# A decoder trunk on one core: first weights into the scan's buffer, the first norm's squares behind the first tiles, both broadcasts of the even mixer placed later

## The chip, the core and the metric

The kernel runs on one core of one Trainium2 chip. Its work is spread over TensorE (PE, with its weight loads shown as PEld), VectorE (DVE), ScalarE (ACT), GpSimd (POOL) and SyncE (SP), which issues most of the DMAs; a few are issued by ACT. Each engine takes its instructions strictly in the order in which they stand in its queue, and waits on semaphores for the others. The metric is the time of one execution in device microseconds.

## The reference, cut to what matters

A two-layer decoder trunk over 256 tokens of width 2048, in float32, batch 1. The first ("even") layer's mixer is where the change lies:

```python
def conv_ssm_mixer(h, w_in, conv_w, ..., w_out):
    z = h @ w_in                                   # 2048 x 4096
    gate_b, gate_c, xa, u = jnp.split(z, ...)      # four parts of 1024
    ya = gate_b * causal_dwconv(gate_c * xa, conv_w)
    ys = s5_branch(u, ...)                         # a complex diagonal scan over the 256 tokens
    return jnp.concatenate([ya, ys], axis=-1) @ w_out

mem_n = rms_norm(mem, norm_mem)                    # 256 memory tokens, used by both layers
for l in range(2):
    h = h + mixer(rms_norm(h, norm_mix[l]))        # even: conv_ssm_mixer, odd: window attention
    h = h + memory_cross_attention(rms_norm(h, norm_xattn[l]), mem_n, w_q, w_kv, w_o)
    h = h + conv_gated_mlp(rms_norm(h, norm_ffn[l]), ...)
return rms_norm(h, norm_final)
```

## The kernel before

All activations are held transposed, 16 slices (k0 to k15) of 128 features by 256 tokens. Matmuls are exact in float32 by splitting: an activation is stored as a pair (high part, rest) side by side in 512 columns, an "op"; a weight is cast by ACT to its high part (`hi`, L90) and DVE subtracts to get the rest (`lo`, L91). One output tile of 128 features is 16 matmuls of `hi` against 512 columns (L105), then 16 of `lo` against 256 (L110). Weights come from memory in pieces of 1 MB into three `raw` buffers; `hi` and `lo` have four buffers each, so two tiles' worth. When a tile is done, `add_halves` copies one half from PSUM on ACT (L160) and adds the other on DVE (L161).

A norm is not applied to the activations before the matmul: the squares of h are summed aside (ACT squares, POOL adds, L172 and L174), PE sums over partitions (L186), DVE takes a reciprocal root in a chain of tiny steps (L194 to L203), builds a diagonal matrix in two halves (L212), PE multiplies it with ones so that every partition gets the factor (L214, the "broadcast"), and ACT copies the result to `rbc` (L216).

The even mixer runs in this order:

- first tiles: the first four output tiles of u (the S5 input) at once, k by k in steps of 1, 1, 2, 2, 2, 4, 4 slices, so that PE can begin when the first slice of x and of the weights `ev_u0` has landed (L259, L262). Squares of h run beside them, four slices late;
- n4 to n7, the other four tiles of u. In n4's follow-up stand the first norm's sum, in n5's its broadcast, then the scaling of u by it (L555), and the splitting of the memory tokens `memT` into ops (16 of them, after n6 and n7);
- for each layer, the memory's keys and values: 16 K tiles (k0 to k15 for layer 0, written k'0 to k'15 here for layer 1), then 16 V steps. K results are gathered four tiles at a time in one buffer, `kst`, and then written to memory by a DMA on ACT's queue (L309). There is one `kst` buffer. Along layer 0's K tiles goes the memory's own norm: tokens loaded after k2, squares after k5 and k6, the reciprocal root after k8, the broadcast after k10;
- 24 gate tiles of w_in, and then the output projection.

The S5 scan (`s5`, four blocks) runs beside all K, V and gate tiles: it is written as a generator, and after each tile `after` lets it emit as many of its steps as a budget per tile allows (S5_US, S5_V, S5_G). A step's heavy rows are DVE's (L493 to L496), ACT's (L489) and a few PE matmuls. The code is written in this order, and a list scheduler turns it into one queue for each engine; the order in the queue is fixed when the program is built. The tile with the tag "S" in the S5 pool has one buffer that holds, one after the other, memT, the memory tokens and the state of every second scan block.

Of the kernel before, what the change touches and what calls it, by code (L numbers as in the profile page):

```python
# [22 lines left out]
P = 128  # L23
# [13 lines left out]
class Trunk:  # L37
# [40 lines left out]
    def wload(self, src, kt, n):  # L78

        nc = self.nc  # L80
        raw = self.rawp.tile([P, kt * n], F32, name="raw", tag="raw")
        nc.sync.dma_start(raw.rearrange("p (k n) -> p k n", n=n), src)
        kc = 1024 // n
        parts = []
        for c in range(0, kt, kc):
            m = min(kc, kt - c)
            hi = self.hip.tile([P, m * n], F32R, name="hi", tag="hi")
            lo = self.lop.tile([P, m * n], F32R, name="lo", tag="lo")
            s = raw[:, c * n:(c + m) * n]
            nc.scalar.copy(hi, s)  # L90
            nc.vector.tensor_tensor(lo, s, hi.bitcast(F32), op=ALU.subtract)  # L91
# [27 lines left out]
    def gemm(self, src, n_tiles, ops, K, evac, late=0, pre=0, mid=None, mid2=None, after=None, one=False, half=None, end=None):  # L119
# [6 lines left out]
        def start(i, k1):  # L126
            n = n_tiles[i]
            w = self.wload(src(n), K, P)
            ps = self.pp.tile([P, 512], F32, name="ps", tag="ps")
# [95 lines left out]
    def setup(self):  # L225
# [15 lines left out]
        def load_x(k0, k1):  # L241
            nc.sync.dma_start(self.hc[:, k0:k1, :], I["xT"][:, k0:k1, :])
        return load_x

    def first_tiles(self, load_x, xs):

        ps = [self.pp.tile([P, 512], F32, name="ps", tag="ps") for _ in range(4)]
        self.stat_begin()
        lag = 4
# [14 lines left out]
        for k in range(KT - lag, KT):  # L264
            self.stat_add(self.h[k])
# [273 lines left out]
    def even_mixer(self):  # L539
# [3 lines left out]
        with tc.tile_pool(name="s5", bufs=1) as pool:  # L543
# [13 lines left out]
            ps = self.first_tiles(load_x, xs)  # L557
# [3 lines left out]

            def load_mem(c):
# [3 lines left out]
            def mem_step(k0, k1):  # L566
                for k in range(k0, k1):
                    self.memop.append(self.split_gain(mem[:, k, :], self.gain(G_MEM, k)))

            def after_u(n):  # L570
                nonlocal rbc
                if n == 4:
                    self.stat_col()
                    load_mem(0)
                elif n == 5:
                    rbc, _ = self.stat_bc()
                    load_mem(1)
                    scale_u(range(0, 6))
                elif n == 6:
                    mem_step(0, 8)  # L580
                    scale_u((6,))
                else:
                    scale_u((7,))
                    mem_step(8, 16)
            rbc = None
            self.gemm(lambda n: win(24 + n), range(4, 8), xs, KT, evac_u, after=after_u)
            r2 = self.smp.tile([P, T], F32, name="r2", tag="r2", bufs=1)
            nc.vector.tensor_tensor(r2, rbc, rbc, op=ALU.mult)
# [4 lines left out]
            def mem_norm(n):  # L593
                if n == 2:
# [4 lines left out]
                elif n in (5, 6):  # L599
                    b = n - 5  # L600
                    nc.scalar.activation(mt["S"][:, b, :], mt["S"][:, b, :], AF.Square, accum_out=mt["ss"][:, b:b + 1])
                elif n == 8:
# [17 lines left out]
            def after_k(n):  # L620
                mem_norm(n)
                after(n)
            self.kv = [self.mem_kv(l, pool, after if l else after_k, after) for l in range(2)]
# [478 lines left out]
```

## Time and profile before

| what | us |
|---|---|
| median of 3 runs | 2818.43 |
| the three runs | 2815.97, 2818.43, 2819.57 |
| the profiled execution | 2817.71 |
| its span, first to last instruction | 2815.9 |
| PE busy in the span | 2785.6 (99%) |
| DVE busy | 1975.3 (70%) |
| ACT busy | 1570.8 (56%) |
| mean granted clock of TensorE | 0.997 |

Where PE is busy nearly all the time, one looks for the places at which it isn't: the list of what PE waits for, and then PE's timeline around the longest entries. An idle time of DVE or ACT costs something only where PE waits for what they bring. A row of a timeline gives the start, the length, the engine and line, what is written and read, the shapes, how many of one kind follow each other, and in brackets the idle time before it and what ended it.

### The profile page before, as it was taken

The page shows a single profiled execution, that of the slowest core. Times are in us where ns is not written, and L with a number is a line of the kernel's source. Part 1 is how long each engine was busy: PE and PEld are TensorE (multiplying, and loading weights), DVE is VectorE, ACT ScalarE, POOL GpSimd, SP SyncE. Part 2 cuts the span into 40 slices and gives each one's busy share as a digit, 9 for nine tenths or more (in the row PEclk, how much of TensorE's full clock was granted, in tenths as well). Part 3 has the DMA queues.
Part 4 walks back from the last instruction along what each step waited for, and adds up shares of the span by engine and source line. Part 5 has one row for each costly group of instructions (what it writes and reads, how often), then busy time and mean ns, then how long its engine had stood idle before and what let it go on. Part 6 is the DMA issues. An engine that isn't in the chain of part 4 may idle for free.

```text
span 2815.9 us, 42249 instructions
## 1 busy us (share of the span) xinstructions
PE 2785.6 (99%) x16263; PEld 2438.2 (87%) x16263; DVE 1975.3 (70%) x3227; ACT 1570.8 (56%) x2544; POOL 360.5 (13%) x397
## 2 busy tenths in 40 slices
PE   9999999999999999999999999999999999999998
PEld 8787878888988888888888888889888888888887
DVE  8978788867666666666666778776666666666666
ACT  7676766655555545545445566555555455454454
POOL 2000000000012211202112310000122022021122
PEclk9999999999999999999999999999999999999999
DMA  8664665555455545455454544454455554554544
GB/s 305 204 213 172 213 226 202 201 181 210 180 177 186 193 171 212 169 206 190 169 210 176 198 171 163 150 211 179 174 185 190 174 205 168 209 192 168 206 171 143
DMA packets 89788, 536.63 MB, mean 191 GB/s; under 512 B 10641, under 2 KB 17137, under 8 KB 38641
## 3 DMA queue, kind: packets, MB, share of 16 engines
q1 hardware_dynamic: 86656, 524.66, 52.7%
q10 hardware_dynamic: 2928, 9.26, 0.9%
q8 instruction: 127, 2.08, 0.3%
q14 instruction: 77, 0.62, 0.1%
HBM read 523.35 MB, written 10.53 MB: 190 GB/s over the span
## 4 chain that ended last, share of the span: by engine, by line
PE 94%; DVE 3%; ACT 2%; DMA 1%; issue 1%; POOL 0%; SPq 0%; DVEq 0%; ACTq 0%; POOLq 0%
PE ps L105 55%; PE ps L110 29%; PE ps L319 2%; PE ps L324 2%; PE ps L320 2%; DVE lo L91 1%; PE m L882 1%; PE m L788 1%; ACT stmp L489 1%; ACT hi L90 1%; DMA kv<-kst 0%; PE m L774 0%; DVE S L494 0%; PE m L742 0%; PE m L852 0%
## 5 line engine op out<-in xcount | busy, mean ns | idle before, releaser
L105 PE MATMUL ps<-op,hi 128*128 128x512 f32 x6997 | 1689.3, 392 | 5.4 <-ACT hi L90 2.8
L105 PEld LDWEIGHTS ps<-op,hi 128*128 128x128 f32 x6997 | 1283.2, 188 | 260.5 <-ACT hi L90 5.2
L91 DVE TENSOR_TENSOR lo<-raw,hi 128x1024 fp32r<-128x1024 f32 (+2 forms) x1033 | 1200.6, 1185 | 378.4 <-ACT hi L90 154.8
L90 ACT CAST hi<-raw 128x1024 fp32r<-128x1024 f32 (+2 forms) x1033 | 1001.8, 983 | 813.0 <-PE ps L105 720.5
L110 PEld LDWEIGHTS ps<-op,lo 128*128 128x128 f32 x7008 | 903.6, 191 | 38.5 <-DVE lo L91 2.3
L110 PE MATMUL ps<-op,lo 128*128 128x256 f32 x7008 | 920.5, 283 | 1.3 <-DVE lo L91 1.3
L172 POOL TENSOR_TENSOR acc<-acc,t 128x256 f32<-128x256 f32 x98 | 90.8, 927 | 1185.7 <-ACT t L174 1181.7
L160 ACT COPY t<-ps 128x256 f32<-128x256 f32 x290 | 106.9, 370 | 166.5 <-PE ps L110 163.6
L919 POOL TENSOR_TENSOR t<-t,rbc 128x256 f32<-128x256 f32 x88 | 68.8, 781 | 748.7 <-DVE t L161 720.9
L922 DVE SCALAR_TENSOR_TENSOR t<-t,ff_conv 128x255 f32<-128x255 f32 x88 | 42.9, 487 | 141.9 <-ACT t L921 141.9
L925 POOL TENSOR_TENSOR t<-t,rbc 128x256 f32<-128x256 f32 x88 | 109.5, 1244 | 216.2 <-ACT t L924 216.2
L68 DVE SCALAR_TENSOR_TENSOR op<-h,gains,op 128x256 fp32r<-128x256 f32 x96 | 72.8, 765 | 85.1 <-ACT op L67 85.0
L489 ACT ACTIVATE stmp<-S,s_pw 128x256 f32<-128x256 f32 (+3 forms) x256 | 116.8, 522 | 27.6 <-DVE S L496 21.6
L75 DVE TENSOR_TENSOR op<-t,op 128x256 fp32r<-128x256 f32 x104 | 43.8, 425 | 118.6 <-ACT op L74 118.2
L161 DVE TENSOR_TENSOR t<-ps,t 128x256 f32<-128x256 f32 x250 | 103.8, 415 | 0.9 <-ACT t L160 0.9
L319 PE MATMUL ps<-hi,op 128*128 128x512 f32 x256 | 101.0, 394 | 0.3 <-ACT hi L90 0.2
L320 PE MATMUL ps<-hi,op 128*128 128x512 f32 x256 | 99.8, 390 | 0.0
L931 POOL TENSOR_TENSOR t<-t 128x256 f32<-128x256 f32 x88 | 67.2, 764 | 135.0 <-DVE t L161 134.7
L74 ACT CAST op<-t 128x256 fp32r<-128x256 f32 x104 | 41.9, 406 | 50.7 <-POOL t L931 43.3
L494 DVE TENSOR_TENSOR S<-S,stmp 128x512 f32<-128x512 f32 (+11 forms) x92 | 60.6, 663 | 13.0 <-ACT stmp L489 12.8
L324 PE MATMUL ps<-lo,op 128*128 128x512 f32 x256 | 63.6, 390 | 0.7 <-DVE lo L91 0.7
L921 ACT ACTIVATE t<-t,ff_b,ff_conv 128x256 f32<-128x256 f32 x88 | 52.3, 595 | 20.7 <-POOL t L919 20.7
(213 smaller groups left out, 1494.9 us busy)
## 6 DMA issues: line engine op xcount, KB each, us to landing
raw<-in_ff_gate SPq DMA_DIRECT2D x88, 1024.0 KB, 4.8
raw<-in_ff_up SPq DMA_DIRECT2D x88, 1024.0 KB, 4.8
raw<-in_ff_down SPq DMA_DIRECT2D x128, 704.0 KB, 4.0
raw<-in_xa_k SPq DMA_DIRECT2D x32, 1024.0 KB, 4.9
raw<-in_xa_v SPq DMA_DIRECT2D x32, 1024.0 KB, 5.3
raw<-in_xa_q SPq DMA_DIRECT2D x32, 1024.0 KB, 4.8
raw<-in_xa_o SPq DMA_DIRECT2D x32, 1024.0 KB, 4.8
raw<-in_ev_w_in SPq DMA_DIRECT2D x28, 1024.0 KB, 4.9
```

Of the source, the lines that this page charges most:

```text
L90: nc.scalar.copy(hi, s)
L91: nc.vector.tensor_tensor(lo, s, hi.bitcast(F32), op=ALU.subtract)
L105: nc.tensor.matmul(ps, lhsT=hi, rhs=o, start=k == 0, stop=False)
L110: self.nc.tensor.matmul(ps[:, :T], lhsT=w[k][1], rhs=ops[k][:, :T], start=False, stop=k == K - 1)
L160: self.nc.scalar.copy(t, ps[:, T:])
L161: self.nc.vector.tensor_tensor(out, ps[:, :T], t, op=ALU.add)
L172: nc.gpsimd.tensor_tensor(self.acc, self.acc, self.sq, op=ALU.add)
L319: nc.tensor.matmul(ps[b], lhsT=o[:, b * P:(b + 1) * P], rhs=w[j][0], start=k == 0, stop=False)
L320: nc.tensor.matmul(ps[b], lhsT=o[:, T + b * P:T + (b + 1) * P], rhs=w[j][0], start=False, stop=False)
L324: nc.tensor.matmul(ps[b], lhsT=self.memop[k][:, b * P:(b + 1) * P], rhs=w[j][1], start=False, stop=k == KT - 1)
L489: nc.scalar.activation(tmp[:, x, :, p - p0, :], at(0, both, p), AF.Copy, scale=pw[:, x, k, 8 * b + p:8 * b + p + 1])
L925: nc.gpsimd.tensor_tensor(y, y, self.rbc, op=ALU.mult)
```

## The change

Four things are done in the even mixer.

- The weights of k0 to k7 of the first tiles land in the S5 pool's "S" tile, which is not in use yet, instead of in the `raw` buffers; so their loads wait for no buffer. x of k0 and k1 is issued by ACT instead of SP.
- The squares of h leave the first tiles. They follow n4 to n7, four in the middle of each; the splitting of memT comes after n5, n6 and n7 instead of n6 and n7, and both loads of memT are issued at once. n4 and n5 accumulate in banks of the other PSUM pool ("m").
- The first norm's sum comes after k0 and its broadcast after k1 of layer 0's K, and all of u is scaled there. The S5 generator starts after k2 instead of k0.
- The memory's norm is moved back by two tiles (loads after k4, squares after k7 and k8, root after k10), and its broadcast goes to layer 1's K, after k'4.

```diff
-    def wload(self, src, kt, n):
+    def wload(self, src, kt, n, raw=None):
-        raw = self.rawp.tile([P, kt * n], F32, name="raw", tag="raw")
+        if raw is None:
+            raw = self.rawp.tile([P, kt * n], F32, name="raw", tag="raw")
...
-            ps = self.pp.tile([P, 512], F32, name="ps", tag="ps")
+            ps = self.pp.tile([P, 512], F32, name="ps", tag="ps") if place is None else place(n)
...
-        def load_x(k0, k1):
-            nc.sync.dma_start(self.hc[:, k0:k1, :], I["xT"][:, k0:k1, :])
+        def load_x(k0, k1, early=False):
+            (nc.scalar if early else nc.sync).dma_start(self.hc[:, k0:k1, :], I["xT"][:, k0:k1, :])
...
-            load_x(k, k + step)
-            w = self.wload(self.I["ev_u0"][:, k:k + step, :], step, 512)
+            load_x(k, k + step, k < 2)
+            w = self.wload(self.I["ev_u0"][:, k:k + step, :], step, 512, room[:, 512 * k:512 * (k + step)] if k < 8 else None)
...
-                if k + j >= lag:
-                    self.stat_add(self.h[k + j - lag])
...
-            ps = self.first_tiles(load_x, xs)
+            ps = self.first_tiles(load_x, xs, place([P, 8 * 512]))
...
+            for c in range(2):
                 nc.sync.dma_start(mem[:, 8 * c:8 * c + 8, :], self.I["memT"][:, 8 * c:8 * c + 8, :])
             self.memop = []
+            self.stat_begin()
+
+            def half_u(n):
+                for k in range(4 * (n - 4), 4 * (n - 3)):
+                    self.stat_add(self.h[k])
+
+            def after_u(n):
+                for k in {4: (), 5: range(0, 5), 6: range(5, 11), 7: range(11, 16)}[n]:
                     self.memop.append(self.split_gain(mem[:, k, :], self.gain(G_MEM, k)))
+            self.gemm(lambda n: win(24 + n), range(4, 8), xs, KT, evac_u, half=half_u, after=after_u,
+                      place=lambda n: self.bank() if n < 6 else self.pp.tile([P, 512], F32, name="ps", tag="ps"))
...
+            def first_norm(n):
                 nonlocal rbc
+                if n == 0:
+                    self.stat_col()
+                elif n == 1:
+                    rbc, _ = self.stat_bc()
+                    scale_u(range(8))
+                    nc.vector.tensor_tensor(r2, rbc, rbc, op=ALU.mult)
...
-                elif n == 10:
-                    self.mrbc, _ = self.stat_bc("mem")
...
             def after_k(n):
+                first_norm(n)
                 mem_norm(n)
+                if n > 1:
+                    after(n)
+
+            def after_k1(n):
+                if n == 4:
+                    self.rcol = self.mcol
+                    self.mrbc, _ = self.stat_bc("mem")
                 after(n)
-            self.kv = [self.mem_kv(l, pool, after if l else after_k, after) for l in range(2)]
+            self.kv = [self.mem_kv(l, pool, after_k1 if l else after_k, after) for l in range(2)]
```

Line numbers shift by a few: the diagonal's rows are L212 before and L213 after, the broadcast L214 and L215, the cast L90 and L91, `lo` L91 and L92, `kst`'s add L161 and L162, the squares L174 and L175.

Three places in the queues. The first is ACT between the first tiles and tile n4; `ps` is the first tiles' sum, `S` holds memT, `h` is x. Before:

```order
L90 CAST hi<-raw 128x1024 [waits DMAHW7_49,DVE_49,PE_49]
L90 CAST hi<-raw 128x1024 [waits DVE_49,PE_49]
L67 ACTIVATE op<-S,gains 128x256 [waits DMAHW0_49]
L67 ACTIVATE op<-S,gains 128x256
L160 COPY t<-ps 128x256 [waits PE_49,Pool_49] x4
L67 ACTIVATE op<-S,gains 128x256 x4
L90 CAST hi<-raw 128x1024 [waits DMAHW1_49,DVE_49]
```

The two casts at the top are tile n4's, the one at the bottom is the first of n5. And now:

```order
L67 ACTIVATE op<-S,gains 128x256 [waits DMAHW0_49]
L67 ACTIVATE op<-S,gains 128x256
L161 COPY t<-ps 128x256 [waits PE_49] x4
L175 ACTIVATE t<-h 128x256 x3
L67 ACTIVATE op<-S,gains 128x256
L91 CAST hi<-raw 128x1024 [waits DMAHW1_49,DVE_49]
L91 CAST hi<-raw 128x1024 [waits DVE_49]
```

The casts at the bottom are n4's: they stand behind the copies, three squares and a gain.

The second place is the memory norm's broadcast on DVE before, in layer 0's K. `S_735` is the scan's state, `lo_1542` and `lo_1546` are weights of tile k12, `kst_1295` takes k10's result, `t_1460` is the diagonal for which PE waits in k11:

```order
L494 TENSOR_TENSOR S_735<-S_735,stmp_1879 128x512 [waits DVE_49]
L495 TENSOR_TENSOR S_735<-S_735,stmp_1879 128x256 [waits DVE_49]
L496 TENSOR_TENSOR S_735<-S_735,stmp_1879 128x256
L493 TENSOR_TENSOR stmp_1999<-S_735,s5_pw_1184 128x256 [waits DVE_49]
L493 TENSOR_TENSOR stmp_1999<-S_735,s5_pw_1184 128x256
L494 TENSOR_TENSOR S_735<-S_735,stmp_1999 128x256 [waits DVE_49]
L91 TENSOR_TENSOR lo_1542<-raw_1539,hi_1541 128x1024 [waits DMAHW4_49,PE_49,Activation_49]
L161 TENSOR_TENSOR kst_1295<-ps_1424,t_1457 128x256 [waits Activation_49]
L212 TENSOR_SCALAR t_1460<-ident_91,rcol_1302 128x128 x2
```

These rows stand there no more; the broadcast's rows on DVE are now in layer 1's K. `kst_2616` gathers k'0 to k'3 and `kst_2854` k'4 to k'7, in the same one buffer; `lo_2889` and `lo_2893` belong to tile k'5, `lo_2935` and `lo_2939` to k'6, and `t_2858` is the diagonal:

```order
L92 TENSOR_TENSOR lo_2889<-raw_2886,hi_2888 128x1024 [waits DMAHW6_49,PE_49]
L92 TENSOR_TENSOR lo_2893<-raw_2886,hi_2892 128x1024 [waits PE_49,Activation_49]
L162 TENSOR_TENSOR kst_2616<-ps_2762,t_2795 128x256 [waits Activation_49]
L490 TENSOR_TENSOR S_1769<-S_1769,stmp_3643 128x2x2x127
L490 TENSOR_TENSOR S_1769<-S_1769,stmp_3685 128x2x2x127 [waits Activation_49]
L491 TENSOR_TENSOR S_1769<-S_1769,stmp_3643 128x2x127 [waits DVE_49]
L492 TENSOR_TENSOR S_1769<-S_1769,stmp_3643 128x2x127
L92 TENSOR_TENSOR lo_2935<-raw_2932,hi_2934 128x1024 [waits DMAHW7_49,PE_49,Activation_49]
L213 TENSOR_SCALAR t_2858<-ident_91,rcol_1390 128x128 [waits Pool_49]
L162 TENSOR_TENSOR kst_2854<-ps_2821,t_2855 128x256 [waits DMAHW3_49,Activation_49]
L213 TENSOR_SCALAR t_2858<-ident_91,rcol_1390 128x128
L92 TENSOR_TENSOR lo_2939<-raw_2932,hi_2938 128x1024
```

The two halves of the diagonal stand on either side of the first write into `kst_2854`, and that row waits for a DMA queue (the write of `kst_2616`).

The third place is PE in tile k'5 of layer 1 (`ps_2896`), where the broadcast now stands behind seven `hi` matmuls:

```order
L106 MATMUL ps_2896<-op_554,hi_2888 128x512
L106 MATMUL ps_2896<-op_557,hi_2888 128x512
L215 MATMUL m_2861<-t_2858,ones_89 128x256 [waits DVE_49]
L106 MATMUL ps_2896<-op_560,hi_2888 128x512
L106 MATMUL ps_2896<-op_563,hi_2892 128x512 [waits Activation_49]
```

Before, these rows of layer 1 held no broadcast; the same pattern stood in layer 0's k11.

More of the change, by code (lines that the diff above doesn't have):

```diff
@@ L117, in mm, with gemm @@
         self.mm_lo(ps, w, ops, k0, k1, K)
-    def gemm(self, src, n_tiles, ops, K, evac, late=0, pre=0, mid=None, mid2=None, after=None, one=False, half=None, end=None):
+    def gemm(self, src, n_tiles, ops, K, evac, late=0, pre=0, mid=None, mid2=None, after=None, one=False, half=None, end=None, place=None):
         n_tiles = list(n_tiles)
@@ L263, in first_tiles @@
             k += step
-        for k in range(KT - lag, KT):
-            self.stat_add(self.h[k])
         return ps
```

33 lines of the change are left out of this document (7 added, 26 removed).

## The prediction

> **What bounds the kernel now.** First the page's list of engines, then two rows of the table of what PE waits for and one of PE's timeline, then a table of stages. The columns of a wait are total us, times and longest; those of a stage are its length, then busy us and instructions of PE, PEld, DVE, ACT and POOL, the granted clock, the busy share of the DMA engines and GB/s.
>
> ```profile
> PE 2785.6 (99%) x16263; PEld 2438.2 (87%) x16263; DVE 1975.3 (70%) x3227; ACT 1570.8 (56%) x2544; POOL 360.5 (13%) x397
> PE m L214 <- DVE t L212: 9.0, 2, 6.3
> PE ps L259 <- ACT hi L90: 2.9, 2, 2.1
> 2806.30 0.70 PE L214 MATMUL m<-t,ones 128*128 128x256 f32 x2 [2.68 <-DVE t L212]
> 10.00:20.00 10.00, 9.21 (x53) 7.88 (x52) 9.02 (x10) 10.00 (x22) 7.30 (x9) 1.00 1.00 373
> 20.00:30.00 10.00, 9.69 (x53) 8.19 (x52) 10.00 (x12) 8.01 (x15) 5.83 (x6) 1.00 0.97 374
> 120.00:130.00 10.00, 3.67 (x12) 2.69 (x11) 9.90 (x18) 1.12 (x3) 0.00 (x0) 0.70 0.33 107
> 140.00:190.00 50.00, 50.00 (x263) 41.79 (x261) 39.30 (x52) 35.80 (x61) 0.00 (x0) 1.00 0.57 195
> 560.00:2815.00 2255.00, 2242.83 (x13232) 1978.70 (x13230) 1505.99 (x2331) 1182.59 (x1878) 345.90 (x376) 1.00 0.52 184
> ```
>
> PE is busy 99% of the span, so the change can win only PE's idle time, or add to it. From 560 us on nothing is touched and PE is busy 2242.8 of 2255 us. All that the change can move lies in the even mixer ahead of that. The largest wait there is the matmul of a broadcast (L214) for its diagonal (L212). The 9.0 us are two waits, 6.33 and 2.68; the second stands at the kernel's end (at 2806.30), so the first norm's broadcast, in tile n6, waits for nothing today. The 6.3 us is the memory norm's. On PE's timeline, and then on DVE's (start, us, instruction, idle before and its releaser):
>
> ```profile
> 119.77 1.78 PE L105 MATMUL ps<-op,hi 128*128 128x512 f32 x7
> 127.87 1.22 PE L214 MATMUL m<-t,ones 128*128 128x256 f32 x2 [6.33 <-DVE t L212]
> 128.53 3.53 PE L105 MATMUL ps<-op,hi 128*128 128x512 f32 x9
> 131.90 2.08 PE L110 MATMUL ps<-op,lo 128*128 128x256 f32 x16
> 124.41 1.06 DVE L493 TENSOR_TENSOR stmp<-S,s_pw 128x256 f32<-128x256 f32 x2
> 127.35 0.47 DVE L212 TENSOR_SCALAR t<-ident,rcol 128x128 f32<-128x128 f32 x2
> 281.01 3.83 PE L105 MATMUL ps<-op,hi 128*128 128x512 f32 x16
> 284.68 2.08 PE L110 MATMUL ps<-op,lo 128*128 128x256 f32 x16
> ```
>
> A normal K tile is the last pair: 284.68 - 281.01 = 3.67 us of hi matmuls (0.16 of the row's 3.83 overlap the next row), and 2.08 - 0.16 = 1.92 of lo, 5.6 in all. Tile k11 began at 119.77 and its lo matmuls ended at 131.90 + 1.92: 14.05 us. Less 5.6 for the tile and 0.26 for the two passes of the broadcast (2.08 / 16 each), its wait costs about 8.2 us: 6.33 of standing still, and the rest in slow matmuls (the nine hi matmuls took 3.53 us where 9/16 of 3.67 is 2.06, so 1.5). Its diagonal is late because DVE takes its instructions in order and scan rows (L493 and the like) of the S5 block stand ahead.
>
> **The change part by part: the old wait.** It is not all won by moving it. The scan of S5 block 0 runs on DVE and ACT from its first to its last row below, and the casts of the weights stand between its rows on ACT.
>
> ```profile
> 55.33 0.17 DVE L340 TENSOR_SCALAR s5p<-s5p 128x32 f32<-128x32 f32 x1
> 177.06 1.06 ACT L90 CAST hi<-raw 128x1024 fp32r<-128x1024 f32 x1
> 179.05 0.39 PE L319 MATMUL ps<-hi,op 128*128 128x512 f32 x1
> 181.97 0.42 DVE L496 TENSOR_TENSOR S<-S,stmp 128x254 f32<-128x254 f32 x1
> 271.65 2.35 PE L110 MATMUL ps<-op,lo 128*128 128x256 f32 x16 [1.28 <-DVE lo L91]
> 277.15 2.11 PE L105 MATMUL ps<-op,hi 128*128 128x512 f32 x8 [1.31 <-ACT hi L90]
> ```
>
> The cast that PE takes at 179.05 ends at 178.12, only 0.93 us ahead, although PE had stood still for 8 us before. If that stall alone went, PE would be 8.2 us earlier at this place and the cast at most 0.9 too early: all but 0.9 us comes back as waits for casts and lo parts. The change also lets the S5 steps begin at k2 instead of k0, two tiles or 11.2 us of PE later, and in the new order block 0 ends two V steps later. Chain end by that: 181.97 + 11.2 + 0.9 for two pairs of diagonal halves (0.47 each) = 194. Two V steps beyond 179.05, each taken as long as a tile of K, PE stands at 190 today. Against the time of before that is between -0.9 (only the margin won) and +4 (194 - 190, all of it to be waited for); I take **+2**, nearer the chain than the margin because the margin is the row that was seen.
>
> **The first tiles.** x for k0 and k1 is now issued by ACT behind its table load and a copy.
>
> ```profile
> 0.74 0.39 SPq L242 DMA_DIRECT2D h<-in_xT  x1
> 2.48 0.19 ACT L235 COPY t<-ones 128x1 f32<-128x1 f32 x1
> 3.44 0.51 ACT L67 ACTIVATE op<-h,gains 128x256 fp32r<-128x256 f32 x1 [0.77 <-DMA gains<-in_gains]
> 4.83 1.20 PE L259 MATMUL ps<-op,hi 128*128 128x512 f32 x4
> 8.62 1.20 PE L259 MATMUL ps<-op,hi 128*128 128x512 f32 x4 [2.12 <-ACT hi L90]
> 11.08 2.09 PE L259 MATMUL ps<-op,hi 128*128 128x512 f32 x8 [0.80 <-ACT hi L90]
> ```
>
> The issue slips from 0.74 to 2.67, about 1.9 us, so the first matmul comes at 6.7 instead of 4.83. That costs nothing, because PE already stands 2.12 us before k1 and 0.80 before k2, waiting for casts of weights. From 10 us on the stage table has the DMA engines full (share 1.00, 373 GB/s): issuing earlier into the landing room lands nothing earlier. The Trainium skill (DMA: Bandwidth & Descriptors, Issuing engines are not separate DMA queues) says the same of the second issuer: transfers of all issuers run on the same 16 engines, and only issue time is saved. By that rule the new issuer gives 0; were it a queue of its own it would give at most SP's 2 x 0.43 us. Moving the squares (L174) behind the first tiles takes POOL's adds out of this stage, and its PE idle time between 10 and 30 us is 0.79 + 0.31 = 1.1: the stage ends at best at 31.43 - 1.1 = 30.3.
>
> ```profile
> 29.52 2.08 PE L262 MATMUL ps<-op,lo 128*128 128x256 f32 x16
> 31.43 0.50 PE L186 MATMUL m<-ones,acc 128*128 128x1 f32 x4
> 33.48 2.79 PE L105 MATMUL ps<-op,hi 128*128 128x512 f32 x11 [1.54 <-DVE u L161]
> 21.99 1.33 ACT L174 ACTIVATE t<-h 128x256 f32<-128x256 f32 x4
> 23.22 3.88 ACT L90 CAST hi<-raw 128x1024 fp32r<-128x1024 f32 x4
> 31.32 1.20 ACT L160 COPY t<-ps 128x256 f32<-128x256 f32 x4 [2.79 <-PE ps L262]
> ```
>
> But before, both casts of tile n4 stood ahead of the four copies. In the new order ACT runs the copies (1.20), three squares (3 x 0.33 = 1.0), a gain (0.51) and only then the first cast (0.97), less 0.1 of overlap: n4 starts 3.6 us behind the end of the stage, at 33.9 instead of 33.48. The tiles n4 and n5 go to other PSUM banks, so the wait for u falls away, but it isn't the last one any more. Value **+0.4**, between -0.5 (stage at 30.3 with the squares behind the cast) and +1.5 (stage still at 31.4). On SP both loads of memT (1 MB each, 2.8 us at 374 GB/s) now stand ahead of n4's weights. These were cast from 23.22 + 2 x 0.97 = 25.2 on (the third of the four casts), so 5.6 us later they have landed by 30.8, and their cast now comes near 33: no cost, and 2 us of cover.
>
> **The first broadcast** moves from n6, where it waited for nothing, into k2 after four matmuls. Its diagonal stands behind two interleaved reciprocal-root chains on DVE. Bounds 0 and 1.5 (the 1.54 us on PE's row at 33.48); **+0.5**.
>
> **The memory broadcast** goes into tile k'5 of the second K (layer 1), after seven matmuls. On DVE its two halves now stand around the row that writes kst for k'4, and this row waits until the kv write of k'0 to k'3 has landed, since kst has one buffer. The same wait in this place today (DVE and the DMA issue on ACT's queue), then the whole line's waits and landings:
>
> ```profile
> 284.59 0.42 DVE L161 TENSOR_TENSOR kst<-ps,t 128x256 f32<-128x256 f32 x1
> 285.05 0.33 ACTq L309 DMA_DIRECT2D kv<-kst  x1
> 293.05 0.43 DVE L161 TENSOR_TENSOR kst<-ps,t 128x256 f32<-128x256 f32 x1 [3.64 <-DMA kv<-kst]
>   DVE kst L161: 11.3, 5
> DMA to landing us min/median/max: 6.4/6.9/7.9
> ```
>
> Today nobody but DVE waits there, as PE has its lo parts. Now PE does. Tile k'5 starts at 281.01; k'3's kst is written at 284.59, its kv write issued at 285.05 and landed at 293.05 (8.0 us). Then 0.34 for kst and half of 0.47 for the second half: the diagonal is ready about 12.7 us after the tile's start. PE wants it after seven matmuls, 7 x 0.23 = 1.6. **Stall 11.1**. Queued behind the matmul on PE is the whole kernel; behind the waiting DVE row is k'6's second lo part. Bounds: if DVE were a tile earlier (kst of k'3 three us ahead of k'5 instead of 3.6 behind) and the landing 6.4 us, 11.1 - 6.6 - 1.6 = 2.9; longer than 12 nothing here shows. The slow matmuls behind it come again, **+1.5**. The Trainium skill (TensorE: Matmul & The Clock Gate, Part 1: The HAM clock gate) says that PE falls to half its clock after an idle window of about 3.4 us and needs as much busy time to come back; the stage table shows 0.70 around the old stall, which agrees. By that rule this term is an estimate of 1.7 instead of 1.5, and the old stall, returned as waits of about 1 us, would come back without its 1.5: block 0 at +0.5 instead of +2.
>
> **The rest of layer 1's K.** PE waits there today for 1.28 and 1.31 us. S5 block 1 sits a little thinner around them in the new order: **-1.5** (0 to -2.6). Blocks 2 and 3 follow later and denser: **+1** (0 to +4).
>
> Sum: 0.4 + 0.5 + 2 + 11.1 + 1.5 - 1.5 + 1 = 15.0. The profiled execution took 2817.71 us, span 2815.9; 2832.7 by this, and the median of the runs stands 0.7 above it: **2833**.
>
> **The rivals.** (1) *Faster*: the old 8.2 us is won in full, and the new broadcast waits 2.9 us. For it: between 140 and 190 us DVE is idle 10.7 of 50 us and ACT 14.2, so both might catch up. Against it: the 0.93 us at 179.05, in spite of that idle time, and the start two tiles later. -8.2 + 2.9 - 0.5 gives 2812. It decides at margins at the first V steps of over 5 us. Chance 0.07. (2) *About the same*: block 0 comes out even, and the kv write is issued earlier and lands in 6.4, a stall of 4 to 6 us, short enough for little slow clock: 0.4 + 0.5 + 5 - 1.5 = 4.4, 2822. For it: DVE gets k'3's kst earlier if scan rows ahead of it are fewer. Chance 0.15. (3) *Slower still*: the late start of S5 isn't made up in any block, +4 and +4, with +1.5 at either end of the first stage and no gain in K: 11.1 + 1.5 + 8 + 3 = 23.6, 2841. For it: 1.28 and 1.31 are already waited for in block 1. Chance 0.18. (4) *The first part doesn't do what it says*: weights land no sooner, since DMA is full; worked above, it is in the forecast's +0.4, and 2 us more if k2 also slips by x's 1.9.
>
> **How the numbers follow.** Forecast 2833 (2825 to 2840) 0.60, and the rivals' 0.07, 0.15, 0.18. A measurement of this kernel tells about 0.2% from no change, 5.6 us, so the bounds are 2812.8 and 2824.1: faster 0.07, same 0.15, slower 0.78. The range takes in the forecast and most of (2) and (3), 2817 to 2845, and leaves out (1), the lower part of (2) and the upper of (3).
>
> **What would show it.** The wait of the matmul L215 for its diagonal L213 in layer 1's k'5, about 11 us, with kst waiting for kv between the two halves; no wait of 6 us in k11; instead several waits of 0.5 to 2 us for casts and lo parts in the last K tiles and the V steps of layer 0; n4 starting at 33.5 to 35; first matmul near 6.7 and k2 near 11. I am wrong if k'3's kst stands a tile earlier than today, if the diagonal halves run together, or if V4 to V7 begin 5 us earlier than today without a wait.

## The result, and the profile after

The changed kernel takes **2834.36 us** (median of 4 runs, 2834.14 to 2834.40) against 2817.88 us of the kernel before beside it: a ratio of 1.0059, with a 95% interval of 1.0041 to 1.0076. It is slower by 16.5 us. The spans of the profiled executions are 2832.6 and 2815.9, so the two traces hold the same difference, 16.7 us.

What PE waits for now, from the table of waits of the changed kernel (total us, times, longest):

```profile
PE m L215 <- DVE t L213: 12.7, 2, 10.0
PE ps L106 <- ACT hi L91: 3.4, 6, 1.5
PE m L106 <- ACT hi L91: 3.2, 1, 3.2
PE ps L320 <- DVE lo L92: 2.1, 3, 1.7
PE ps L111 <- DVE lo L92: 1.8, 2, 1.0
PE ps L315 <- ACT hi L91: 1.6, 3, 0.9
```

The broadcast's wait was 6.33 us and is 10.0 (the other 2.7 of the first row is the kernel's end, as before). New are one wait of 3.2 us at the first matmul of n4 (it writes an "m" bank), and five short ones for `lo` in K and V tiles of layer 0 (L111, L320); two of the six L106 waits, 0.86 and 0.30 us, stand in layer 0's K too, and those of L315 in layer 1's V steps. The stages of the changed kernel, with the same columns as before:

```profile
10.00:20.00 10.00, 10.00 (x50) 8.58 (x49) 8.74 (x14) 8.52 (x17) 0.00 (x0) 1.00 1.03 420
20.00:30.00 10.00, 10.00 (x56) 8.72 (x56) 8.49 (x17) 6.96 (x15) 0.00 (x0) 1.00 1.01 424
30.00:60.00 30.00, 26.82 (x149) 23.45 (x148) 20.75 (x27) 23.15 (x43) 13.17 (x15) 0.94 0.66 244
120.00:130.00 10.00, 10.00 (x61) 8.91 (x60) 7.92 (x12) 6.53 (x13) 0.00 (x0) 1.00 0.74 259
140.00:190.00 50.00, 45.67 (x226) 35.73 (x225) 46.65 (x91) 28.28 (x47) 0.00 (x0) 0.97 0.52 178
230.00:300.00 70.00, 59.14 (x309) 48.12 (x308) 59.04 (x113) 42.71 (x72) 0.00 (x0) 0.93 0.50 172
```

Between 120 and 130 us, where PE stood for 6.3 us, it is now fully busy; between 140 and 190, where it was fully busy, it loses 4.3 us; between 230 and 300 it is busy 59.1 us, 7.8 less than the 66.97 of before. The place of the new wait, on PE's timeline of the changed kernel and then on DVE's and ACT's:

```profile
283.89 1.89 PE L106 MATMUL ps<-op,hi 128*128 128x512 f32 x7 [0.42 <-ACT hi L91]
295.83 1.22 PE L215 MATMUL m<-t,ones 128*128 128x256 f32 x2 [10.05 <-DVE t L213]
296.49 3.87 PE L106 MATMUL ps<-op,hi 128*128 128x512 f32 x9
```

```profile
288.03 0.41 DVE L162 TENSOR_TENSOR kst<-ps,t 128x256 f32<-128x256 f32 x1
288.36 1.27 DVE L490 TENSOR_TENSOR S<-S,stmp 128x508 f32<-128x508 f32 x2
289.56 0.41 DVE L491 TENSOR_TENSOR S<-S,stmp 128x254 f32<-128x254 f32 x1
289.89 0.41 DVE L492 TENSOR_TENSOR S<-S,stmp 128x254 f32<-128x254 f32 x1
290.22 1.21 DVE L92 TENSOR_TENSOR lo<-raw,hi 128x1024 fp32r<-128x1024 f32 x1
291.36 0.28 DVE L213 TENSOR_SCALAR t<-ident,rcol 128x128 f32<-128x128 f32 x1
295.15 0.42 DVE L162 TENSOR_TENSOR kst<-ps,t 128x256 f32<-128x256 f32 x1 [3.52 <-DMA kv<-kst]
295.50 0.28 DVE L213 TENSOR_SCALAR t<-ident,rcol 128x128 f32<-128x128 f32 x1
```

```profile
288.48 0.33 ACTq L305 DMA_DIRECT2D kv<-kst  x1
```

PE is ready for the broadcast at 295.83 - 10.05 = 285.8. The first half of the diagonal is only made at 291.36, 5.6 us later, behind scan rows and `lo`. The second half stands behind the add into `kst`, which waits until the kv write issued at 288.48 has landed, at about 295.1.

How much later (or, with a minus, earlier) each tile begins on PE than in the kernel before, in us, read from the starts of the tiles' first matmuls in the two traces. The S5 matmuls (about 1 us) stand between other tiles in each kernel, which makes steps of 1 us; the stages are read where several tiles agree:

| tile | n4 | n5 | k4 | k11 | k12 | k14 | V0 | V2 | V4 | V8 | V12 | k'5 | k'6 | k'15 | end |
|---|---|---|---|---|---|---|---|---|---|---|---|---|---|---|---|
| changed kernel | 1.8 | 3.4 | 2.9 | 4.0 | -4.5 | -2.6 | 0.3 | 3.0 | 5.3 | 5.6 | 5.8 | 2.9 | 15.5 | 15.5 | 16.7 |

So the removed wait wins 8.5 us from k11 to k12, and all of it and 1.4 us more are gone again by V4. 2.9 us were lost before that, by k4; 2.9 are won between V12 and k'5; 12.6 are lost in k'5.

The table compares one execution with one other, and the first stage differs between executions. In the kernel before and the four kernels below that leave its first tiles as they are, n4 began at 33.48, 33.83, 33.85, 33.85 and 34.00 us; in the changed kernel and the three below with its first tiles, at 35.26, 34.35, 34.50 and 34.75. The table pairs the earliest of the first with the latest of the second: by the means n4 begins 0.9 us later instead of 1.8, and k4 1.9 instead of 2.9. The other terms are steps within an execution, which this touches less.

### The profile page after: what moved, and what is told of

Read it like the earlier page. It is cut to its first block, busy times and chain, and to the rows that moved or that the text cites. A ratio compares the mean times of both kernels' runs of the same rounds, so it can differ in the third digit from the quotient of the medians.

```text
span 2832.6 us, 42236 instructions
## 1 busy us (share of the span) xinstructions
PE 2794.6 (99%) x16263; PEld 2442.7 (86%) x16263; DVE 1973.1 (70%) x3227; ACT 1572.1 (55%) x2544; POOL 359.3 (13%) x397
## 3 DMA queue, kind: packets, MB, share of 16 engines
q8 instruction: 127, 2.08, 0.3%
## 4 chain that ended last, share of the span: by engine, by line
PE 86%; DVE 2%; ACT 1%; issue 0%; POOL 0%; DVEq 0%; POOLq 0%; ACTq 0%
PE ps L106 52%; PE ps L111 27%; PE m L881 1%; PE ps L315 1%; PE ps L316 1%; PE ps L320 1%; DVE lo L92 1%; PE m L787 1%; ACT stmp L485 1%; PE m L773 0%; PE m L741 0%; PE m L851 0%; DVE S L490 0%; PE m L850 0%; PE m L849 0%
## 5 line engine op out<-in xcount | busy, mean ns | idle before, releaser
L106 PE MATMUL ps<-op,hi 128*128 128x512 f32 x6965 | 1682.7, 392 | 4.8 <-ACT hi L91 3.4
L106 PEld LDWEIGHTS ps<-op,hi 128*128 128x128 f32 x6965 | 1277.3, 188 | 259.7 <-ACT hi L91 6.8
L92 DVE TENSOR_TENSOR lo<-raw,hi 128x1024 fp32r<-128x1024 f32 (+1 forms) x1028 | 1195.7, 1186 | 387.9 <-ACT hi L91 147.0
L91 ACT CAST hi<-raw 128x1024 fp32r<-128x1024 f32 (+1 forms) x1028 | 998.3, 983 | 833.3 <-PE ps L106 722.5
L111 PEld LDWEIGHTS ps<-op,lo 128*128 128x128 f32 x6976 | 899.5, 191 | 38.8 <-DVE lo L92 2.7
L111 PE MATMUL ps<-op,lo 128*128 128x256 f32 x6976 | 916.2, 283 | 1.8 <-DVE lo L92 1.8
L161 ACT COPY t<-ps 128x256 f32<-128x256 f32 x288 | 106.0, 370 | 168.3 <-PE ps L111 164.0
L485 ACT ACTIVATE stmp<-S,s_pw 128x256 f32<-128x256 f32 (+3 forms) x256 | 117.1, 523 | 17.0 <-DVE S L492 11.2
L162 DVE TENSOR_TENSOR t<-ps,t 128x256 f32<-128x256 f32 x250 | 103.9, 416 | 0.6 <-ACT t L161 0.6
L315 PE MATMUL ps<-hi,op 128*128 128x512 f32 x256 | 101.8, 398 | 1.8 <-ACT hi L91 1.6
L490 DVE TENSOR_TENSOR S<-S,stmp 128x512 f32<-128x512 f32 (+11 forms) x92 | 61.0, 667 | 15.0 <-ACT stmp L485 14.8
L320 PE MATMUL ps<-lo,op 128*128 128x512 f32 x256 | 64.7, 394 | 2.1 <-DVE lo L92 2.1
```

What stands on the lines that cost most here:

```text
L106: nc.tensor.matmul(ps, lhsT=hi, rhs=o, start=k == 0, stop=False)
L111: self.nc.tensor.matmul(ps[:, :T], lhsT=w[k][1], rhs=ops[k][:, :T], start=False, stop=k == K - 1)
L161: self.nc.scalar.copy(t, ps[:, T:])
L162: self.nc.vector.tensor_tensor(out, ps[:, :T], t, op=ALU.add)
L315: nc.tensor.matmul(ps[b], lhsT=o[:, b * P:(b + 1) * P], rhs=w[j][0], start=k == 0, stop=False)
L320: nc.tensor.matmul(ps[b], lhsT=self.memop[k][:, b * P:(b + 1) * P], rhs=w[j][1], start=False, stop=k == KT - 1)
```

## The experiments

Twelve kernels, each timed against the kernel before in three rounds. The times are medians.

### 1. Is the old wait lost time, or does it stand in the scan's shadow?

A wait of PE stands in the shadow of other engines when PE, coming earlier without it, would only wait later for what those engines bring. The kernel before, with only the memory norm's broadcast moved to behind the last gate tile, where nobody waits for it:

```diff
-                elif n == 10:
-                    self.mrbc, _ = self.stat_bc("mem")
...
             for _ in bg:
                 pass
+            self.rcol = self.mcol
+            self.mrbc, _ = self.stat_bc("mem")
```

> The kernel before with only the memory norm's broadcast (diagonal, matmul, copy) moved from behind layer 0's k10 to behind the last gate tile, where nothing reads it for long. So the old wait of 6.3 us in k11 (8.2 us with the slow matmuls) is gone and no other part of the change is there. Theory A (the scan of S5 block 0 on DVE and ACT sets the end of that stretch, the wait only stood in its shadow): k12 starts 8.4 us earlier, but waits for casts and lo parts in k13 to V6 take back all but 0.9 us; time 2817.0. Theory B (the wait was lost time and comes back in full): 2809.7. A short wait for the diagonal at the mixer's end, up to 2 us, may add to either.

Measured: 2817.61 us, ratio 1.0000 (0.9991 to 1.0009). Theory A holds, and no part of the 8.2 us was won. The wait of 6.3 us is gone from the list; in its place stand short waits, three of them on PE's timeline of this kernel:

```profile
144.11 1.22 PE L110 MATMUL ps<-op,lo 128*128 128x256 f32 x8 [2.10 <-DVE lo L91]
150.14 1.22 PE L110 MATMUL ps<-op,lo 128*128 128x256 f32 x8 [1.16 <-DVE lo L91]
151.61 1.22 PE L110 MATMUL ps<-op,lo 128*128 128x256 f32 x8 [0.25 <-DVE lo L91]
```

They are 3.5 us together; the rest stands in the V steps. k12 begins 8.1 us earlier than in the kernel before, V0 3.4, V2 1.1, and V4 0.3 us later. The last scan row of block 0 ends at 183.56 us, against 182.38 in the kernel before: that PE came 8 us earlier did not end the scan of block 0 earlier.

### 2. Does the new wait stand in a shadow too?

The changed kernel with the broadcast moved to the same late place:

```diff
             def after_k1(n):
-                if n == 4:
-                    self.rcol = self.mcol
-                    self.mrbc, _ = self.stat_bc("mem")
                 after(n)
...
             for _ in bg:
                 pass
+            self.rcol = self.mcol
+            self.mrbc, _ = self.stat_bc("mem")
```

> The changed kernel with only the memory norm's broadcast moved from layer 1's k'4 to behind the last gate tile. Theory A2 (block 1 of the scan is nearly over in k'5, so the new wait of 10.0 us and its slow matmuls, 12.6 together, stand in nobody's shadow): 2834.4 - 12.6 = 2821.8. Rival R (as in layer 0, most of a wait that goes comes back as waits for casts): 2829 to 2833.

Measured: 2821.96 us, 12.4 less than the changed kernel, as theory A2 has it (1.0014 of the kernel before, 1.0005 to 1.0023). k'6 begins 2.8 us later than in the kernel before, k'15 2.9: nothing of the 12.6 us is taken back. In layer 0 PE ran ahead of a scan block that went on for more than 50 us; in this kernel block 1's last scan row ends at 296.9, some 8 us after k'6 begins at 289.35, and from there to k'15 PE waits for nothing but 0.24 us. That the nearly finished block is the reason fits these rows, but no run tests it.

### 3. What makes the new wait: the kv write, or DVE's order?

First the broadcast one tile earlier, where no row that waits for kv stands ahead of the diagonal:

```diff
-                if n == 4:
+                if n == 3:
```

> The changed kernel with the memory norm's broadcast one tile earlier, behind layer 1's k'3 instead of k'4. Both halves of the diagonal then stand together behind lo of k'5's first part and ahead of the kst row of k'3, which waits for no kv write. Theory K (the landing of the kv write makes the wait, as in the prediction): without it the broadcast in k'4 waits 2 us at most, no slow matmuls; 2834.4 - 10.6 = 2824. Theory Q (DVE comes two tiles late to anything in its queue here, and the kv write is only the last part of the wait): the row ahead of the diagonal ended at 287.0 in the trace of the changed kernel, PE would be there at 277.3 + 1.6 = 278.9, so it waits 8 to 9 us; 2832 to 2834.

Measured: 2830.68 us, 3.7 less than the changed kernel. On PE's and DVE's timelines:

```profile
287.38 1.22 PE L215 MATMUL m<-t,ones 128*128 128x256 f32 x2 [8.76 <-DVE t L213]
```

```profile
285.71 1.22 DVE L92 TENSOR_TENSOR lo<-raw,hi 128x1024 fp32r<-128x1024 f32 x1
286.85 0.48 DVE L213 TENSOR_SCALAR t<-ident,rcol 128x128 f32<-128x128 f32 x2
```

The wait of 8.8 us is the one that theory Q gives, with no kv write in it; the time is 1.3 us under Q's range. Up to k'4 the tiles begin when they do in the changed kernel (both 3.45 us later than before); tiles k'4 and k'5 together then lose 9.3 us here and 12.1 there. Theory K falls. Then the kernel before with the broadcast moved as the change moves it, and nothing else:

> The kernel before with only the memory norm's broadcast moved behind layer 1's k'4, as the change has it. Here both halves stand together ahead of the kst row that waits for the kv write. Theory A with Q: in the trace of before the row ahead of the diagonal ends at 288.3 and PE would be there at 281.0 + 1.6 = 282.6, a wait of 6 us and 1.5 of slow matmuls; with 0.9 won in layer 0, 2824.5. Theory A with K: a wait of 2 us at most, 2817 to 2819. Theory B with Q: 2817.9 - 8.2 + 7.5 = 2817.2; B with K: 2811.

Measured: 2826.75 us (1.0031, 1.0019 to 1.0044). On PE's and DVE's timelines:

```profile
287.86 1.22 PE L214 MATMUL m<-t,ones 128*128 128x256 f32 x2 [6.61 <-DVE t L212]
```

```profile
287.33 0.47 DVE L212 TENSOR_SCALAR t<-ident,rcol 128x128 f32<-128x128 f32 x2
290.96 0.42 DVE L161 TENSOR_TENSOR kst<-ps,t 128x256 f32<-128x256 f32 x1 [3.15 <-DMA kv<-kst]
```

The broadcast waits 6.61 us, again with both halves of the diagonal together and ahead of the `kst` row, and k'6 is 9.3 us later against the kernel before than k'5 was. This is A with Q; the time is 2 us above its number, as the tile lost 9.3 us instead of 7.5 (twelve slow hi matmuls behind the wait took 4.79 us, 2.0 more than 12/16 of 3.67, and V4 began only 0.1 us earlier). This single edit is 8.7 of the 16.5 us.

Last, the changed kernel with the kv wait taken away: `kst` holds two tiles and has two buffers, in the same space.

```diff
-            if n % 4 == 0:
-                cur["k"] = kvp.tile([P, 4, T], F32, name="kst", tag="kst")
-            self.add_halves(cur["k"][:, n % 4, :], ps)
-            if n % 4 == 3:
-                nc.scalar.dma_start(kv[n // 4][:, :1024], cur["k"].rearrange("p a b -> p (a b)"))
+            if n % 2 == 0:
+                cur["k"] = kvp.tile([P, 2, T], F32, name="kst", tag="kst", bufs=2)
+            self.add_halves(cur["k"][:, n % 2, :], ps)
+            if n % 2 == 1:
+                c0 = 512 * (n % 4 // 2)
+                nc.scalar.dma_start(kv[n // 4][:, c0:c0 + 512], cur["k"].rearrange("p a b -> p (a b)"))
...
-            vs = kvp.tile([P, 2, 512], F32, name="kst", tag="kst")
             for b in range(2):
-                nc.scalar.activation(vs[:, b, :], ps[b], AF.Copy, scale=self.mcol[:, b:b + 1])
-            nc.scalar.dma_start(kv[c][:, 1024:], vs.rearrange("p a b -> p (a b)"))
+                vs = kvp.tile([P, 512], F32, name="kst", tag="kst", bufs=2)
+                nc.scalar.activation(vs, ps[b], AF.Copy, scale=self.mcol[:, b:b + 1])
+                nc.scalar.dma_start(kv[c][:, 1024 + 512 * b:1536 + 512 * b], vs)
```

> The changed kernel with kst as two buffers of two tiles each instead of one of four, so that no add into kst waits for the kv write ahead of it (V's results likewise in two halves). Theory A3: of the new broadcast's wait of 10.0 us in k'5, about 6 are DVE's order (the first half of the diagonal came 6 us late by itself) and 4 the kv write with kst and the second half behind it; the wait becomes 6 us, and DVE's waits for kv in layer 0 (some 5 us) no longer lengthen the scan, worth 0 to 4 us: 2826 to 2830. Theory K (the kv write makes the wait): 1 to 3 us of wait, 2820 to 2823.

Measured: 2824.87 us, 9.5 less than the changed kernel (1.0024 of the kernel before, 1.0014 to 1.0034). The broadcast's wait, on PE's timeline, and the rows ahead of the diagonal on DVE's:

```profile
287.59 1.22 PE L215 MATMUL m<-t,ones 128*128 128x256 f32 x2 [6.38 <-DVE t L213]
```

```profile
284.06 1.28 DVE L491 TENSOR_TENSOR S<-S,stmp 128x508 f32<-128x508 f32 x2
285.25 0.42 DVE L492 TENSOR_TENSOR S<-S,stmp 128x254 f32<-128x254 f32 x1
285.58 0.42 DVE L493 TENSOR_TENSOR S<-S,stmp 128x254 f32<-128x254 f32 x1
285.92 1.22 DVE L92 TENSOR_TENSOR lo<-raw,hi 128x1024 fp32r<-128x1024 f32 x1
287.05 0.48 DVE L213 TENSOR_SCALAR t<-ident,rcol 128x128 f32<-128x128 f32 x2
```

The wait is 6.38 us without any kv write ahead, as theory A3 has it: of the 10.05, about 6.4 are DVE's order and 3.7 the kv write. The time fell by more than those 3.7, as the rest of the even mixer got faster too (k'5 begins 3.9 us earlier than in the changed kernel, 0.9 of it already at n4); the next runs are about that.

### 4. What does the single kst buffer cost the scan's chain?

Experiment 1's kernel with two `kst` buffers:

> The kernel before with the memory norm's broadcast behind the last gate tile (as in the run before) and kst in two buffers of two tiles. Theory A (in layer 0's K PE runs in the shadow of the scan chain on DVE and ACT): DVE's idle times for kv in that chain, 1.63 at 92.7 and 1.93 at 114.4 in the trace of before, go, so the waits in k13 to V4 shrink by about 3.5, and those in k'3 and k'4 (1.28 and 1.31) shrink as well: 2812 to 2814.5. Rival: the chain hangs on ACT and on the scan's own order, DVE's idle time there is no part of it: 2817 to 2818.

Measured: **2809.18 us**, 0.9969 of the kernel before (0.9958 to 0.9980). Theory A, and more than it asked: 8.4 us less than experiment 1. Before, the table of DVE's waits had 5 waits for kv, and here it has none; the row of the kernel before:

```profile
DVE kst L161 <- DMA kv<-kst: 11.3, 5, 3.8
```

Block 0's scan, from its first L494 to its last L496 row, took 85.7 us in the kernel before and 86.6 in experiment 1; here it takes 72.5, and DVE's idle time within it falls from 13.5 (experiment 1) to 4.4 us. The tiles: V4 begins 5.0 us earlier than in experiment 1, k'5 7.3. Three of DVE's five waits, 5.2 us in experiment 1's kernel, stood in layer 0 and the other two in layer 1. The queues are planned anew for the two buffers, so not all of the 14 us is idle time that was removed, and no run tells the removed waits from the new order.

To tell this from the moved broadcast, the kernel before with nothing but the two buffers:

> The kernel before with nothing but kst in two buffers of two tiles; the memory norm's broadcast is back behind layer 0's k10. Theory A: without DVE's waits for kv (1.63 and 1.93 ahead of it) the diagonal comes 3 to 4 us earlier, so PE waits 2.5 to 3.5 us in k11 instead of 6.3, and that still lies in the scan chain's shadow; the time is that of the run with the broadcast at the end, 2809 to 2811. Rival (what PE waits in k11 is lost, the gain came from the moved broadcast): 2812 to 2817.

Measured: 2812.11 us (0.9978, 0.9969 to 0.9987), at the lower end of the rival's range and 1.1 us above theory A's. The wait in k11 fell less than forecast:

```profile
126.56 1.10 PE L214 MATMUL m<-t,ones 128*128 128x256 f32 x2 [4.84 <-DVE t L212]
```

In this queue the halves stand around an add into `kst` that waits for nothing and takes 0.42 us; the first half is made only at 125.70, 4.0 us after PE is ready, behind scan rows and `lo`. Against experiment 4's first kernel k12 is 7.2 us later, V2 and all behind it 3.8. So of 7.2 us lost in k11 only 3.4 are taken back here, where experiment 1 showed that all 8.1 were. That the wait counts in part once the scan of block 0 is shorter fits this, but the order of the queues differs too. Neither theory is right alone, and some of the gain of experiment 4's first kernel comes from the moved broadcast.

### 5. The first tiles

Experiment 2's kernel with memT loaded behind the weights of n4 and n5:

```diff
-            for c in range(2):
-                nc.sync.dma_start(mem[:, 8 * c:8 * c + 8, :], self.I["memT"][:, 8 * c:8 * c + 8, :])
...
             def half_u(n):
+                if n < 6:
+                    c = n - 4
+                    nc.sync.dma_start(mem[:, 8 * c:8 * c + 8, :], self.I["memT"][:, 8 * c:8 * c + 8, :])
```

With that, the casts of n4 stand ahead of the four copies and the squares on ACT's queue.

> The changed kernel with the broadcast behind the last gate tile (2822.0 in that run) and memT loaded behind n4's and n5's weights instead of ahead of them; ACT's queue then has n4's casts ahead of the four copies and the squares. Theory P (the order on ACT costs the 3.2 us wait of n4 and the 1.6 us of slow matmuls behind it): n4 starts right behind the first tiles, k0 4 to 5 us earlier; since the scan's first steps follow k2, the chain moves with it: 2817 to 2818. Rival C (the chain doesn't move with PE, so what n4 wins comes back as waits in k13 to V6): 2820 to 2822.

Measured: 2816.54 us (0.9995, 0.9986 to 1.0005), 5.4 less than experiment 2. Theory P holds; the time is 0.5 us below its range. The changed kernel's end of the first tiles and start of n4, and then this kernel's:

```profile
30.01 2.07 PE L260 MATMUL ps<-op,lo 128*128 128x256 f32 x16
35.26 5.53 PE L106 MATMUL m<-op,hi 128*128 128x512 f32 x16 [3.18 <-ACT hi L91]
```

```profile
29.13 2.08 PE L260 MATMUL ps<-op,lo 128*128 128x256 f32 x16
31.04 3.82 PE L106 MATMUL m<-op,hi 128*128 128x512 f32 x16
```

n4 begins 2.4 us earlier than in the kernel before instead of 1.8 later (1.3 later in experiment 2's kernel), and its 16 matmuls take 3.82 us instead of 5.53. With the chain's start tied to k2, V4 keeps most of it: 1.7 us earlier than before, where experiment 2 had 4.7 later.

All three edits together:

> All three together on the changed kernel: broadcast behind the last gate tile, memT behind n4's and n5's weights, kst in two buffers. If P and A both hold: 2813 to 2815, ahead of the kernel before. If the chain doesn't move with PE: 2818.

Measured: **2808.80 us**, 0.9971 of the kernel before (0.9960 to 0.9981): ahead of both kernels, below the expected range, and as fast as experiment 4's first kernel. The change's own first part then brings n4 3.0 us ahead of the kernel before, but little of that lasts: experiment 4's first kernel, which has the old first part, begins n4 3.3 us later than this one and V4 only 0.3 us later, and the two times differ by 0.4 us.

With x of k0 and k1 issued by SP again:

```diff
-            load_x(k, k + step, k < 2)
+            load_x(k, k + step)
```

> The run with all three edits (2808.8), and x of k0 and k1 issued by SP again, as before the change. The prediction's step (the DMA engines are full, so who issues is nothing; first matmul 2 us earlier, k2 and all behind it as they were): 2808.3 to 2809.3. Rival (PE's first matmuls come 2 us earlier and the rest follows): 2806.8.

Measured: 2810.82 us (0.9975, 0.9964 to 0.9986; its seven runs spread from 2808.57 to 2813.70). In the trace the first matmul comes at 4.91 instead of 6.77, and n4 within 0.02 us of the run before; so the rival, by which all that follows comes 2 us earlier, falls. The agreement to 0.02 us is chance: with the same first tiles n4 began between 30.53 and 31.30 us in the kernels above and below. The median lies above both expectations, 2 us over the run before; the intervals of the two ratios overlap, and this was not followed up.

### 6. When the S5 generator starts

The kernel with all three edits, with the generator started one tile earlier, and one later:

```diff
-                if n > 1:
+                if n > 0:
                     after(n)
```

> The run with all three edits (2808.8), and the S5 generator started behind k1 instead of k2. Theory A (block 0's chain sets the end of that stretch, and its late start is what the change lost there, +2 in the prediction): PE's waits from k15 to V4, 6.0 us in the run before, shrink by 2 to 5 us: 2804 to 2807. Rival (the chain hangs on u's scaling behind the first broadcast in k2, so the earlier call moves nothing): 2808 to 2809.5.

> The run with all three edits (2808.8), and the S5 generator started behind k3 instead of k2. The start behind k1 ended block 0 of the scan later (180.6 against 178.6 us) and cost 4.4 us, so the tile at which the generator starts works by how its rows fall between the weights' rows, and not by its date. If later is better in the same way: 2805 to 2808. If k2 is just a good fit and any other start costs: 2810 to 2815.

Measured: 2813.19 us from k1 and 2811.15 us from k3. From k1 both theories miss. Block 0's scan began at 103.9 instead of 106.1 and ended at 180.6 instead of 178.6. From k3 it ended at 194.3, and yet V8 began 1.7 us earlier than from k2; the loss comes in later blocks. The start from k3 falls into the range expected if k2 is just a good fit, but its 2.4 us are hardly more than the 2 us between experiment 5's last two kernels. A loss is shown only for k1, where 0.8 of the 4.4 us stand already at n4, ahead of the generator. That the later start as such loses time, as the prediction argued for block 0, isn't shown: from k3 block 0 ended 15.7 us later and V4 began 2.4 us earlier. So the end of the block alone doesn't set when PE gets its V weights; what does, in the order of the rows, stays open.

## Why the prediction was right

**What bounds the kernel, and the old wait.** Both steps hold. Experiment 1 took the wait away alone and won nothing: all 8.1 us came back between k13 and V4, as waits for `lo` and casts; 0.9 was forecast to stay and none is seen. The rival that had the 8.2 us won in full is refuted for this kernel. The reason that the prediction gave, the end of block 0's scan, is only in part borne out (experiments 4 and 6).

**The memory broadcast.** Forecast 11.1 of waiting and 1.5 of slow matmuls; measured 10.05, and 3.87 - 2.06 = 1.8 of slow matmuls; by the tiles' starts 12.6 in all, which is the forecast's sum. The place, the rows and the releaser are those forecast. That the sum fits to 0.1 us is luck: the wait came out 1 us short, and the missing part is made up by the broadcast's own two passes, 0.66 us on PE, which the forecast left out, and by the slow matmuls. Within the wait two errors partly cancel: `kst` of k'3 came 4.1 us behind the tile's start instead of 3.6, and the kv write landed after 6.7 us instead of 8.0. And the weight was put on the kv write; experiment 3 shows that DVE's order alone makes 6.4 of the 10, and that the wait would be there (6.6) without any kv write ahead of it.

**Block 0.** Forecast +2, measured 5.8 - 2.9 = +2.9 from k4 to V12, within its bounds; its cause, the later start, isn't shown (part 6). The working behind it was off: block 0's first heavy row (L490 there, L494 before) came at 115.8 us instead of 96.7, so 19.1 later and not the 11.2 of two tiles, and the block ended at 199.8 instead of the forecast's 194. The prediction's upper bound, the end of the block less 190, would then be +9.8; +2.9 was measured, so the block's end is not what sets it.

**The first tiles.** This term was mis-sized: forecast +0.4 at n4, between -0.5 and +1.5; measured +1.8 at n4 and +2.9 at k4 in the two traces, +0.9 and +1.9 by the means given under the result. The step from the end of the stage to n4 was right (3.6 forecast, 3.34 measured, by copies, squares, gain and cast as listed). Wrong were two others. The stage ended at 31.92 (its last lo matmuls begin at 30.01 and take 1.91) instead of 30.3: PE had no idle time in it any more between 10 and 30 us, as forecast, but its first eight hi matmuls ran at little over half their speed (2.08 and 1.91 us for four, 1.20 before). And the prediction priced the 3.2 us in which PE stood, but not the slow matmuls behind them (5.53 us for 16, 3.82 otherwise: 1.7). The slow start differs from execution to execution (last section), so about 1 us of this term is chance. The claim that the DMA engines were full and could land nothing earlier was wrong as well: they moved 420 GB/s between 10 and 20 us where they had moved 373. And the first matmul came near the forecast 6.7, at 6.73, by luck: x was issued at 1.24 instead of 2.67, but its split (L67) stood on ACT's queue behind the casts of k0's and k1's weights and began only at 5.46.

**The first broadcast** waited for nothing (its bounds were 0 and 1.5, +0.5 was taken). **Layer 1's K**: -2.9 against -1.5, just outside its bounds (0 to -2.6); the two waits of 1.28 and 1.31 us ahead of k'5 shrank to 0.17 and 0.15. **Later blocks**: 16.7 - 15.5 = +1.2 against +1.

The terms measured, 2.9 (first tiles and first broadcast), 2.9, 12.6, -2.9 and 1.2, sum to 16.7, where the prediction had 15.0. The errors of the other terms are +2.0 (the first tiles and the first broadcast), +0.9, -1.4 and +0.2; they partly cancel and are small against the one large term, and that was sized by one row: the same DVE row waiting for the same write, seen in the kernel before, where it hurt nobody. The prediction gives two ranges, 2825 to 2840 and 2817 to 2845; the measured time lies in both.

## What to carry to other kernels

A wait that ends in a long stretch where another engine is the bound need not be time to be won: look how early the next things come that PE takes from that engine (0.93 us here) before anything is moved. A small row (a diagonal of 0.28 us) that PE will wait for must not be put into a queue behind rows that wait for a transfer or belong to a scan; read what stands ahead of it in that queue, with its releasers. And the idle time of the engine that PE waits for is where to look instead: a single staging buffer, for which DVE had waited five times, was split in two in the same space, and that won 8.4 us with the broadcast out of the way and 5.8 with it in its old place.

## What the runs showed of the hardware that was not expected

- PE's speed right after the start differs between executions that hold the same matmuls. The first four hi matmuls of the changed kernel and of experiment 5's first kernel:

```profile
6.73 2.08 PE L257 MATMUL ps<-op,hi 128*128 128x512 f32 x4 [1.47 <-DVE op L68]
```

```profile
6.88 1.20 PE L257 MATMUL ps<-op,hi 128*128 128x512 f32 x4 [1.61 <-DVE op L68]
```

  Both follow the same warm-up matmuls and about 1.5 us of idle time; the granted clock of the window from 0 to 10 us is 1.00 in the changed kernel, although its matmuls took nearly twice as long. In experiment 3's last kernel four matmuls at 8.63 us took 2.08 us as well, and there the window from 9 to 12 us shows a granted clock of 0.56. The kernel before had an idle time of 2.12 us ahead of k1 and no slow matmuls behind it; in experiment 4's second kernel, with the same first tiles, the first four hi matmuls took 2.05 us. What decides it isn't shown.
- In this trace ACT's DMA issue did not wait for its table load: x was issued at 1.24 us, while the load ran from 1.18 to 2.46; the prediction had put the issue behind it, at 2.67.

```profile
1.18 1.28 ACT L236 ACT_TABLE_LOAD   x1 [1.18 <-PEq L1090]
1.24 0.87 ACTq L243 DMA_DIRECT2D h<-in_xT  x2
```

- The kv write of 512 KB landed after 2.8 to 6.9 us in the changed kernel (median 6.7) and 6.4 to 7.9 before (median 6.9). The 2.8 is a single one of eight; the write in the place of the new wait had taken 7.9 before, which is why the forecast for it was too long.
